# New tokens' scores of a hybrid decoder step, taken out of sixteen decode turns into two blocks of eight heads; value products and the last gate blocks rearranged

## The chip, the cores and the metric

The kernel runs on one core of a Trainium2 chip, in one launch. The metric is device time in microseconds of that core. The engines are TensorE (PE, its weight loads PEld), VectorE (DVE), ScalarE (ACT), GpSimd (POOL) and SyncE (SP), which issues nearly all transfers; instructions on one engine's queue run in their order.

## The reference, cut to what matters

The program is one inference step: a recurrent layer, then a forgetting-attention layer, for a prompt of 2048 tokens and for 8 samples with 8 new tokens each. A sample has 4096 past tokens in 32 cache pages and 16 heads of 64. Its attention is over past and new tokens together:

```
k_all = concat([past_k, k_new]); v_all = concat([past_v, v_new]); c_all = cumsum(logf_all)
s = einsum('bqhd,bkhd->bhqk', q, k) * HEAD_DIM ** -0.5
s = s + cq - ck                       # sums of the log forget gates
s = where(k_pos <= q_pos, s, -inf)
p = softmax(s);  o = einsum('bhqk,bkhd->bqhd', p, v)
y = (o * silu(g)) @ w_out             # q and g come from x @ w_in
```

So each sample has, besides its scores against the cache, an 8x8 block of scores of its new tokens against each other, for each head, with a causal mask.

## The kernel before, in words

The prompt goes through the recurrent layer in two chunks (phase_a1, phase_a2) and through the projections to k, v, q and gate in three (phase_b: 1024, 512 and 512 tokens). Projections of 256 columns are the kv matmuls (token_major) and the qg matmuls (feature_major); every product is three float32r matmuls. The 64 new tokens ride in the first chunk. Their keys and values are stored to DRAM (ks_d, vs_d), their queries too (qs_d), and sample_c stores their forget sums (cn_d).

Decode against the cache is cut into 16 turns, one for a sample and eight heads (DB = 8 samples, 2 groups). The first two turns run beside the projections of the first chunk, the other fourteen beside the projections of the last two chunks and then beside the prompt's attention. Generators yield estimated costs, and Side.along draws decode forward by the cost of the work that it runs beside; a scheduler with a simulated time line then orders each engine's instructions, so the place in the source does not alone decide the place on a queue. The pages come by SyncE (pages, four pages of 256 KB to one raw buffer, four such buffers in the second decode), are transposed on VectorE into ktr (L1193), and meet the queries on TensorE (scores, L1161); the score bank dS is one PSUM bank, tag d. Their sums are subtracted (sc) and the maximum taken.

In the middle of a turn, new_scores (L1169) does the same for the new tokens: the eight key rows lie in rawn (L1116), are transposed into a tile kx that in the second decode is borrowed from the raw ring (spare, shown as sy), 16 matmuls of 8 columns go to a dS bank (L1176), and two VectorE operations take the sums (cn, L1153) off and add the mask maskN; a third takes the maximum (L1182).

Later in the turn the values follow: products (L1275) multiplies four value pages, together keeping the eight matmuls of a buffer in one run, and new_products (L1283) adds the new tokens' rows one tick later, into the same PSUM tile dO. A copy ob is then gathered by four matmuls with the selector sel (L1303, dres).

The gate blocks come last in the last chunk: tanh on ACT (L975) and a product on DVE (L976) into one of two tiles tgb, then a store to sg_d (L977); the last two blocks' stores (cc == 3, that is rows r = 6 and 7) are issued on ACT's queue, all others on SyncE's. Behind them attention opens its PSUM banks (sx, st, ops) over those of the projections, and takes the weight slots (wkept, tags wh0 to wl2) for its accumulators and exponentials.

Of the kernel before, what the change touches and what calls it, by code (L numbers as in the profile page):

```python
# [11 lines left out]
F32 = mybir.dt.float32  # L12
# [3 lines left out]
ALU = mybir.AluOpType  # L16
# [72 lines left out]
def tile_hawk_fox(  # L89
# [102 lines left out]
    c_d = dt_("cd", [2, 4, 4, DB, NPG // 4, 256])  # L192
    cn_d = dt_("cnd", [H, NSAMP])


# [680 lines left out]
    def phase_b(s, x, feed, nk, early, order, opening=None):  # L876
# [7 lines left out]
        with ExitStack() as es:  # L884
# [62 lines left out]
            def feature_major(kind, cc):  # L947

                W = feed.take()
                for fb in range(2):  # L950
                    r = cc * 2 + fb
                    for c0, nn in s.groups:
# [6 lines left out]
                        if kind == "q":  # L959
                            th = pool.tile([P, 512], F32R, name="qth", tag="fth", bufs=2)  # L960
                            tl = pool.tile([P, 512], F32R, name="qtl", tag="ftl", bufs=2)
                            A.mul(th[:, :nn], ps[:, :nn], 0.125)
                            V.scalar_tensor_tensor(tl[:, :nn], ps[:, :nn], 0.125, f(th[:, :nn]),
                                                   op0=ALU.mult, op1=ALU.subtract)
                            S.dma_start(qd_d[r * P:(r + 1) * P, 0, pt:pt + w], f(th[:, so:nn]))
                            S.dma_start(qd_d[r * P:(r + 1) * P, 1, pt:pt + w], f(tl[:, so:nn]))
                            if so:
                                qf = pool.tile([P, NSAMP], F32, name="qf", tag="qf")
                                A.mul(qf[:, :], ps[:, :so], 0.125)
                                for qd in range(4):  # L970
                                    S.dma_start(qs_d[:, :, qd, r, :].rearrange("b j q -> j b q"),
                                                qf[qd * 32:(qd + 1) * 32, :].rearrange("j (b q) -> j b q", b=DB))
                        else:
                            tg = pool.tile([P, 512], F32, name="tgb", tag="tgb", bufs=2)
                            A.activation(tg[:, :nn], ps[:, :nn], AF.Tanh, scale=0.5)  # L975
                            V.scalar_tensor_tensor(tg[:, :nn], tg[:, :nn], 1.0, ps[:, :nn], op0=ALU.add, op1=ALU.mult)  # L976
                            (A if s is scb[-1] and cc == 3 else S).dma_start(sg_d[r * P:(r + 1) * P, pt:pt + w], tg[:, so:nn])  # L977
                            if so:
                                cp(G, sgs[:, r, :], tg[:, :so])
# [24 lines left out]
    def sample_c(pool, lf):  # L1004
# [14 lines left out]
        S.dma_start(cn_d[:, :], cn[:, :])  # L1019

    def drain(gen):
        for _ in gen:
            pass
# [32 lines left out]
    def decode(es, turns, nraw, nktr, ahead):  # L1056
        pool = sbuf(es, "dec", "right")
        maskN = pool.tile([DS, DS], F32, name="maskN")
        G.memset(maskN[:, :], 0.0)
        G.affine_select(maskN[:, :], maskN[:, :], pattern=[[-1, DS]], compare_op=ALU.is_ge, fill=NEG, base=0,  # L1060
                        channel_multiplier=1)
        qmask = pool.tile([P, DS], F32, name="qmask")
# [49 lines left out]

        def new_rows(rows, b, hg):

            assert known >= {("k" if rows is ks_d else "v", hg * 2 + c) for c in range(2)}
            S.dma_start(rawn[:DS, :], rows[b * DS:(b + 1) * DS, hg * 512:(hg + 1) * 512])  # L1116
            return rawn
# [25 lines left out]
        def keys(t, xs):  # L1143
# [24 lines left out]

            def new_scores(raw):  # L1169
                kx = (spare() if ahead else pool.tile([P, 512], F32, name="kx", tag="kx"))[:, :512]  # L1170
                V.transpose(kx, raw[:, :])
                sp = bank("dS")

                def score(h, x):
                    blk = (h * 2 + x) * 32
                    return T.matmul(sp[:32, h * DS:(h + 1) * DS], qw[:, h // 2, h % 2 * 2 + x, :], kx[:, blk:blk + DS],  # L1176
                                    start=(x == 0), stop=(x == 1))

                together([partial(score, h, x) for h in range(8) for x in range(2)])
                tt(V, t.cn[:, :, :], sp[:DS, :64].rearrange("p (h j) -> p h j", h=8), t.cn[:, :, :], ALU.subtract)  # L1180
                tt(V, t.cn[:, :, :], t.cn[:, :, :], maskN[:, :].unsqueeze(1).to_broadcast([DS, 8, DS]), ALU.add)
                V.tensor_reduce(gmx[:DS, 2, :], t.cn[:, :, :], axis=AX.X, op=ALU.max)  # L1182

            for x in xs:
# [78 lines left out]
        def values(t, xs):  # L1263
# [6 lines left out]

            def products(i, raw, came):

# [5 lines left out]

                together([partial(mm, d, a) for d in range(4) for a in range(2)], came, True)

            def new_products(raw):
                for a in range(2):
                    T.matmul(op[a * 32:(a + 1) * 32, :256], pc[:, a * 32:(a + 1) * 32], raw[:, a * 256:(a + 1) * 256],  # L1283
                             start=False, stop=True)

            for x in xs:
                raw, came = t.raws.pop(0) if t.raws else pages(cache_v, b, hg, x)
                dl.after(2 if ahead and x == 0 else 1, lambda i=x * 4, raw=raw, came=came: products(i, raw, came))
                if x == 5:
                    t.rown = new_rows(vs_d, b, hg)  # L1290
# [10 lines left out]
            sp = bank("dres")  # L1301
            for pr in range(4):
                T.matmul(sp[:, pr * 16:(pr + 1) * 16], ob[:, pr % 2 * P:(pr % 2 + 1) * P], sel[:, pr * 16:(pr + 1) * 16],  # L1303
                         start=True, stop=True)
            for h2 in range(2):
# [623 lines left out]
    te1.close()  # L1929
    stage.close()  # L1930
    dec, last = ExitStack(), ExitStack()

# [56 lines left out]
```

## Time and profile before

| what | us |
|---|---|
| three runs | 2989.36, 2994.17, 2994.76 |
| median | 2994.17 |
| profiled execution, its own time | 2990.82 |
| its span, first to last instruction | 2989.1 |
| mean granted TensorE clock | 0.975 |

The page says busy time for each engine, then the chain of work that ended last. A row of the timeline has the start, the duration, the engine, the line, the operation with out<-in, the count, and in brackets how long the engine was idle before it and what ended that. Names are those of tiles; attention's accumulators and exponentials read atth and attl.

### The profile page before, as it was taken

The numbers are of one execution on the slowest core, as the hardware profiler recorded it, in microseconds if no ns is written. First come the engines' busy times: TensorE is split into PE (matmuls) and PEld (weight loads), VectorE is DVE, ScalarE is ACT, GpSimd is POOL, SyncE is SP. The second block draws the span as 40 slices with busy tenths as digits, with TensorE's granted clock in tenths as the row PEclk, the third lists the DMA queues.
The fourth block names the chain that finished last, engine by engine and source line by source line (L and its number), as shares of the span: only waits on it lengthen the run. The fifth ranks groups of instructions, "written<-read, shape, count | busy, mean of one in ns | idle before, by whom it ended". The sixth has DMA issues, their size and how long they took to land.

```text
span 2989.1 us, 60353 instructions
## 1 busy us (share of the span) xinstructions
PE 2794.3 (93%) x21614; PEld 2242.9 (75%) x21614; DVE 1800.4 (60%) x4013; ACT 1266.8 (42%) x2874; POOL 1079.5 (36%) x1198
## 2 busy tenths in 40 slices
PE   5998999999999999999899899989999999899998
PEld 5997789989999987888877665556656666555687
DVE  7877456435257774766554676666766666655344
ACT  4666342222236664443233345344544445355321
POOL 1654111000015541100001265646665666558422
PEclk9999999999999999999999899999999999999999
DMA  4224536789832246899999979887888998773343
GB/s 124 80 89 135 172 122 180 240 259 282 256 98 75 80 154 189 270 316 356 332 323 315 315 228 287 281 267 254 278 297 269 296 283 258 264 256 109 97 149 111
DMA packets 472536, 653.65 MB, mean 219 GB/s; under 512 B 91192, under 2 KB 268601, under 8 KB 464764
## 3 DMA queue, kind: packets, MB, share of 16 engines
q1 hardware_dynamic: 471660, 647.17, 68.0%
q8 instruction: 171, 2.80, 0.4%
q0 software_dynamic: 288, 2.10, 0.3%
q14 instruction: 129, 1.06, 0.1%
q10 hardware_dynamic: 288, 0.52, 0.0%
HBM read 514.09 MB, written 135.16 MB: 217 GB/s over the span
## 4 chain that ended last, share of the span: by engine, by line
PE 45%; DMA 21%; DVE 6%; ACT 4%; SPq 4%; issue 3%; POOL 1%; DVEq 0%; ACTq 0%; POOLq 0%
DMA raw<-in_cache_k_dram 6%; PE ops L1678 6%; PE st L1650 3%; PE sx L1420 3%; PE dO L1275 3%; PE y L384 3%; PE y L385 3%; PE y L386 3%; DMA raw<-in_cache_v_dram 3%; PE st L1651 2%; PE dS L1161 2%; SPq L1106 2%; PE qg L384 2%; PE kv L386 2%; PE kv L385 2%
## 5 line engine op out<-in xcount | busy, mean ns | idle before, releaser
L1193 DVE STREAM_TRANSPOSE ktr<-raw 128x1024 f32<-128x1024 f32 x256 | 307.8, 1225 | 91.2 <-DMA raw<-in_cache_k_dram 78.8
L1422 DVE TENSOR_REDUCE mxs<-sx 128x1 f32<-128x512 f32 x384 | 254.1, 681 | 146.6 <-PE sx L1420 145.4
L384 PE MATMUL kv<-wh,xh 128*128 128x256 f32 (+3 forms) x1088 | 309.4, 288 | 7.7 <-ACT wh L429 5.7
L385 PE MATMUL kv<-wl,xh 128*128 128x256 f32 (+3 forms) x1088 | 309.9, 287 | 2.8 <-DVE wl L430 2.5
L386 PE MATMUL kv<-wh,xl 128*128 128x256 f32 (+3 forms) x1088 | 309.2, 286 | 0.4 <-DMA xl<-xld 0.4
L1665 ACT ACTIVATE atth<-st 128x512 f32<-128x512 f32 (+3 forms) x312 | 171.6, 557 | 208.6 <-PE st L1653 97.1
L1665 ACT ACTIVATE attl<-st 128x512 f32<-128x512 f32 (+3 forms) x300 | 149.7, 507 | 225.7 <-PE st L1651 121.6
L429 ACT ACTIVATE wh<-wst,gv 128x256 fp32r<-128x256 f32 (+1 forms) x384 | 164.5, 499 | 184.6 <-DMA wst<-in_b_w_in_dram 72.4
L430 DVE SCALAR_TENSOR_TENSOR wl<-wst,gv,wh 128x256 fp32r<-128x256 f32 (+1 forms) x384 | 170.7, 494 | 108.5 <-ACT wh L429 108.4
L384 PE MATMUL qg<-xh,wh 128*128 128x384 f32 (+2 forms) x640 | 230.0, 360 | 1.9 <-ACT wh L429 1.9
L385 PE MATMUL qg<-xl,wh 128*128 128x512 f32 (+2 forms) x640 | 228.6, 358 | 0.0
L386 PE MATMUL qg<-xh,wl 128*128 128x384 f32 (+2 forms) x640 | 226.6, 356 | 0.0
L109 POOL TENSOR_TENSOR atth<-atth,atth 128x512 f32<-128x512 f32 (+2 forms) x143 | 168.8, 1180 | 148.6 <-PE ops L1678 82.5
L384 PEld LDWEIGHTS kv<-wh,xh 128*128 128x128 f32 (+1 forms) x1088 | 203.1, 188 | 14.0 <-ACT wh L429 6.4
L385 PEld LDWEIGHTS kv<-wl,xh 128*128 128x128 f32 (+1 forms) x1088 | 203.3, 188 | 8.7 <-DVE wl L430 4.5
L386 PEld LDWEIGHTS kv<-wh,xl 128*128 128x128 f32 (+1 forms) x1088 | 204.5, 188 | 3.4 <-issue 2.6
L109 POOL TENSOR_TENSOR atth<-atth,attl 128x512 f32<-128x512 f32 (+3 forms) x162 | 167.3, 1033 | 41.7 <-PE ops L1678 22.6
L1126 POOL TENSOR_TENSOR qw<-qb,amask 128x128 f32<-128x128 f32 x64 | 31.1, 491 | 411.1 <-PE dS L1161 298.2
L109 POOL TENSOR_TENSOR attl<-attl,atth 128x512 f32<-128x512 f32 (+3 forms) x111 | 129.4, 1166 | 101.0 <-PE ops L1678 63.3
L1275 PE MATMUL dO<-raw,sx 128*32 128x256 f32 x2048 | 139.6, 393 | 27.0 <-DMA raw<-in_cache_v_dram 18.4
L1426 DVE CUSTOM_DVE_ANT_0 sx<-sx,maskb 128x128 f32<-128x128 f32 (+3 forms) x256 | 122.8, 488 | 57.9 <-PE sx L1420 57.3
L919 ACT COPY kf<-kv 128x256 f32<-128x256 f32 (+1 forms) x136 | 49.0, 366 | 226.1 <-PE kv L386 183.3
(354 smaller groups left out, 7519.2 us busy)
## 6 DMA issues: line engine op xcount, KB each, us to landing
raw<-in_cache_k_dram SPq DMA_DIRECT2D x512, 256.0 KB
raw<-in_cache_v_dram SPq DMA_DIRECT2D x512, 256.0 KB
wst<-in_w_kv_dram SPq DMA_DIRECT2D x48, 512.0 KB
wst<-in_b_w_in_dram SPq DMA_DIRECT2D x48, 512.0 KB
xt<-in_x_prompt_dram SPq DMA_DIRECT2D x32, 512.0 KB
wst<-in_a_w_in_dram SPq DMA_DIRECT2D x64, 256.0 KB
out_dram<-kf SPq DMA_DIRECT2D x128, 128.0 KB
sc<-cd SPq DMA_DIRECT2D x16, 1024.0 KB
```

The costliest lines, as they stand in the source:

```text
L109: eng.tensor_tensor(out, a, b, op=op)
L384: T.matmul(ps, lh(k), rh(k), start=(k == 0), stop=False)
L385: T.matmul(ps, lh(k), rl(k), start=False, stop=False)
L386: end = T.matmul(ps, ll(k), rh(k), start=False, stop=(k == nk - 1))
L429: A.activation(wh[:, k, :], st[:, k, :], AF.Copy, scale=gk)
L430: V.scalar_tensor_tensor(wl[:, k, :], st[:, k, :], gk, f(wh[:, k, :]), op0=ALU.mult, op1=ALU.subtract)
L1193: behind("V", V.transpose(t.kts[pp][:, n], raw[:, :, pp * 256:(pp + 1) * 256]).ins)
L1275: return T.matmul(op[c:c + 32, :256], sx[:, d, i // 4, a * 4:(a + 1) * 4, :].rearrange("p h q -> p (h q)"), raw[:, d, a * 256:(a + 1) * 25 ...
L1422: r = V.reduce_max(mx[:, j, ck:ck + 1], ps[:, :w], axis=AX.X)
L1426: V.tensor_tensor_reduce(ps[:, :w], ps[:, :w], maskb[:, 512 - w:], scale=1.0, scalar=NEG, op0=ALU.add, op1=ALU.max, accum_out=mx[:, j, ck: ...
L1665: pair.append((k, lo, p, A.activation(p[:, lo:], ps[:, lo:], AF.Exp)))
L1678: return T.matmul(ops[r * HD:(r + 1) * HD, a0 * P:], vvs[h % 2][:, k, :], p[:, :].rearrange("p (a r c) -> p a r c", a=2, r=2)[:, a0:, r, : ...
```

## The change

It does four things.

1. among_new(pool, hg), new, makes the scores of all 64 new tokens among each other for eight heads: eight transposes of the key rows, eight 64x64 matmuls with the queries (which are now stored once more, as qn_d), the sums off, the mask on, and the result to DRAM (sn_d). It runs once ahead of the first decode (hg 0, three steps of the projections beside it) and once ahead of the second (hg 1, three further steps). Of the 64x64 block only the samples' 8x8 diagonals are read. In a turn, fetch_c loads its 8x8 blocks from sn_d where it loaded the sums, and only the maximum stays; new_scores, kx, maskN and the load of key rows go.
2. The new tokens' value products are the last two matmuls of the run of the last page buffer.
3. The gather takes two matmuls of 32 columns in place of four of 16.
4. The gate blocks with cc == 3 of the last chunk write a tile tgl each, in the weight slot that has been free longest, and their stores go to SyncE.

```diff
+    qn_d, sn_d = dt_("qnd", [D, NSAMP]), dt_("snd", [2, NSAMP, H // 2, NSAMP])
...
+                                S.dma_start(qn_d[r * P:(r + 1) * P, :], qf[:, :])
...
-                            tg = pool.tile([P, 512], F32, name="tgb", tag="tgb", bufs=2)
+                            if opening and cc == 3:
+                                free, i = wslots[0]
+                                tg = free.tile([P, 4 * WC], F32, name="tgl", tag=f"w{'hl'[fb]}{i}")[:, :512]
+                            else:
+                                tg = pool.tile([P, 512], F32, name="tgb", tag="tgb", bufs=2)
...
-                            (A if s is scb[-1] and cc == 3 else S).dma_start(sg_d[r * P:(r + 1) * P, pt:pt + w], tg[:, so:nn])
+                            S.dma_start(sg_d[r * P:(r + 1) * P, pt:pt + w], tg[:, so:nn])
...
+    def among_new(pool, hg):
+
+        h0 = hg * 8
+        kn = pool.tile([NSAMP, 512], F32, name="kn")
+        S.dma_start(kn[:, :], ks_d[:, hg * 512:(hg + 1) * 512])
+        qt = pool.tile([HD, 8, NSAMP], F32, name="qnt")
+        S.dma_start(qt[:, :, :], qn_d[hg * 512:(hg + 1) * 512, :].rearrange("(h d) t -> d h t", d=HD))
+        sn = pool.tile([NSAMP, 8, NSAMP], F32, name="sn")
+        S.dma_start(sn[:, :, :], cn_d[h0:h0 + 8, :].unsqueeze(0).to_broadcast([NSAMP, 8, NSAMP]))
...
+        yield
+        ps = tpp("knt")
+        for h in range(8):
+            T.transpose(ps[:HD, h * NSAMP:(h + 1) * NSAMP], kn[:, h * HD:(h + 1) * HD], ident[:NSAMP, :NSAMP])
+        kt = pool.tile([HD, 8, NSAMP], F32, name="knt")
+        V.tensor_copy(kt[:, :, :].rearrange("d h t -> d (h t)"), ps[:HD, :])
+        yield
+        ps = tpp("snp")
+        for h in range(8):
+            T.matmul(ps[:NSAMP, h * NSAMP:(h + 1) * NSAMP], qt[:, h, :], kt[:, h, :], start=True, stop=True)
+        tt(V, sn[:, :, :], ps[:NSAMP, :].rearrange("q (h t) -> q h t", h=8), sn[:, :, :], ALU.subtract)
+        tt(V, sn[:, :, :], sn[:, :, :], causal[:, :].unsqueeze(1).to_broadcast([NSAMP, 8, NSAMP]), ALU.add)
+        S.dma_start(sn_d[hg], sn[:, :, :])
+        yield
...
-                S.dma_start(t.cn[:, :, :], cn_d[hg * 8:(hg + 1) * 8, b * DS:(b + 1) * DS].unsqueeze(0).to_broadcast([DS, 8, DS]))
+                sl = slice(b * DS, (b + 1) * DS)
+                S.dma_start(t.cn[:, :, :], sn_d[hg, sl, :, sl])
...
-                    t.rown = new_rows(ks_d, b, hg)
...
-                        new_scores(t.rown)
+                        V.tensor_reduce(gmx[:DS, 2, :], t.cn[:, :, :], axis=AX.X, op=ALU.max)
...
+                mms = [partial(mm, d, a) for d in range(4) for a in range(2)]
+                if rown is not None:
+                    mms += [partial(new, a) for a in range(2)]
+                together(mms, came, True)
...
-            dl.after(1, lambda: new_products(t.rown))
...
-            for pr in range(4):
-                T.matmul(sp[:, pr * 16:(pr + 1) * 16], ob[:, pr % 2 * P:(pr % 2 + 1) * P], sel[:, pr * 16:(pr + 1) * 16],
-                         start=True, stop=True)
+            for e in range(2):
+                to, of = (x[:, :64].rearrange("p (a e c) -> p e a c", a=2, e=2)[:, e] for x in (sp, sel))
+                T.matmul(to, ob[:, e * P:(e + 1) * P], of, start=True, stop=True)
...
+    steps(gen, max(0, 36 - done))
+    done = max(done, 36)
+    with ExitStack() as es:
+        for _ in among_new(sbuf(es, "new_0", "right"), 0):
+            steps(gen, 1)
+            done += 1
...
+    with ExitStack() as es:
+        for _ in among_new(sbuf(es, "new_1", "right"), 1):
+            steps(gen, 1)
```

The orders below name a line, an operation, out<-in and its shape; x16 is a run of so many equal rows.

TensorE in a turn beside attention, before: the new tokens' scores (L1176) between the scores st and the maxima sx of attention.

```order
8973 L1650 MATMUL st<-qa_18035,atth 128x512
8974 L1651 MATMUL st<-attl,atth 128x512
8975 L1176 MATMUL dS<-sy,qw 32x8 x16
8976 L1420 MATMUL sx<-atth,qbt_18033 128x512
8977 L1420 MATMUL sx<-atth,qbt_18033 128x384
```

In the changed kernel the new block stands among the projections ahead of the first decode; here its transposes (knt), with the 72 kv matmuls of 128 tokens that end in these rows ahead of them:

```order
2624 L385 MATMUL kv<-wh,xh 128x256
2625 L386 MATMUL kv<-wl,xh 128x256
2626 L387 MATMUL kv<-wh,xl 128x256
2627 L1044 MATMUL knt<-ident,kn 64x64 x8
2628 L385 MATMUL kv<-wh,xh 128x256
```

The runs on dS of 8 columns are in no turn any more, and knt and snp each stand twice in the program.

ScalarE at the joint of projections and attention, before:

```order
927 L975 ACTIVATE tgb<-qg 128x512 x3
928 L1441 ACTIVATE qbt_18034<-mps,st_p 4x128 x4
929 L977 DMA sgd<-tgb 128x512
930 L975 ACTIVATE tgb<-qg 128x512
931 L977 DMA sgd<-tgb 128x512
932 L1665 ACTIVATE atth_19624<-st 128x512
```

And the same place in the changed kernel:

```order
915 L981 ACTIVATE tgl<-qg 128x512
916 L1459 ACTIVATE qbt_17878<-mps,st_p 4x128 x4
917 L981 ACTIVATE tgl<-qg 128x512
918 L981 ACTIVATE tgb<-qg 128x512 x2
919 L1459 ACTIVATE qbt_17879<-mps,st_p 4x128 x4
920 L1683 ACTIVATE atth_19404<-st 128x384
```

The two stores have left ScalarE's queue, and the blocks with tiles of their own stand ahead of the two blocks that came before them.

More of the change, by code (lines that the diff above doesn't have):

```diff
@@ L1167, in scores @@
                 V.tensor_reduce(gmx[:, g, pp * 4:(pp + 1) * 4], sv, axis=AX.XY, op=ALU.max)
[L1169 to L1182, printed above, removed]
             for x in xs:
@@ L1269, in values, with products @@
             op = t.op
-            def products(i, raw, came):
+            def products(i, raw, came, rown=None):
                 def mm(d, a):
@@ L1277, in mm, with new @@
                                     start=(i + d < 2), stop=(i + d == NPG - 1))
[L1279 to L1284, printed above, removed]
+                def new(a):
+                    return T.matmul(op[a * 32:(a + 1) * 32, :256], pc[:, a * 32:(a + 1) * 32],
+                                    rown[:, a * 256:(a + 1) * 256], start=False, stop=True)
+                mms = [partial(mm, d, a) for d in range(4) for a in range(2)]
+                if rown is not None:
+                    mms += [partial(new, a) for a in range(2)]
+                together(mms, came, True)
             for x in xs:
                 raw, came = t.raws.pop(0) if t.raws else pages(cache_v, b, hg, x)
[L1288 removed]
                 if x == 5:
[L1290 removed]
+                    t.rown = new_rows(b, hg)
+                dl.after(2 if ahead and x == 0 else 1,
+                         lambda i=x * 4, raw=raw, came=came, rown=t.rown if x == 7 else None: products(i, raw, came, rown))
                 yield 2 * PV
```

15 lines of the change are left out of this document (8 added, 7 removed).

## The prediction

> **What bounds the kernel now.** I read the page first, then the busy times by stretch, then TensorE's own waits. The page gives the engines and the chain that ended last:
>
> ```profile
> PE 2794.3 (93%) x21614; PEld 2242.9 (75%) x21614; DVE 1800.4 (60%) x4013; ACT 1266.8 (42%) x2874; POOL 1079.5 (36%) x1198
> ...
> PE 45%; DMA 21%; DVE 6%; ACT 4%; SPq 4%; issue 3%; POOL 1%; DVEq 0%; ACTq 0%; POOLq 0%
> ```
>
> TensorE (PE) is busy 93% of the span, and the chain stays on it longest. The 21% on DMA asks for a look by stage. The stretches below are the first two decode turns (500 to 800 us), the rest of the projections with decode beside them (1240 to 1700), and attention with decode beside it (1700 to 2680). Columns: length, busy us of PE, weight loads, DVE, ACT and POOL, then granted clock, DMA share, GB/s.
>
> ```profile
> 500.00:800.00 300.00, 290.24 (x2807) 275.62 (x2806) 119.25 (x223) 79.31 (x212) 7.89 (x28) 0.99 0.83 254
> 1240.00:1700.00 460.00, 429.08 (x3956) 365.98 (x3958) 278.09 (x550) 157.88 (x412) 29.84 (x46) 0.96 1.00 327
> 1700.00:2680.00 980.00, 920.21 (x8506) 586.32 (x8498) 642.07 (x1369) 440.56 (x1097) 588.21 (x565) 0.97 0.85 272
> ```
>
> PE works 93 to 97% of all three. DMA is full only from 1240 to 1700; in attention it has 15% of 980 us, 147 us, to spare. So I take PE as the bound, with DMA close behind in the middle stage. PE's waits that the change touches (total us, times, longest):
>
> ```profile
> PE dO L1275 <- DMA raw<-in_cache_v_dram: 18.4, 14, 3.8
> ...
> PE sx L1420 <- DVE tgb L976: 6.1, 1, 6.1
> ...
> PE dS L1176 <- DVE sc L109: 4.7, 3, 2.5
> ...
> PE st L1650 <- DVE tgb L976: 1.6, 1, 1.6
> ...
> PE dS L1161 <- DVE cn L109: 0.8, 1, 0.8
> ```
>
> **New tokens' scores, removed from the turns.** Each of 16 turns runs 16 small matmuls on L1176, which the trace counts as 32 passes, 512 in all. One turn's, in attention:
>
> ```profile
> 1783.88 0.39 PE L1650 MATMUL st<-qa,atth 128*128 128x512 f32 x1
> 1784.10 0.39 PE L1651 MATMUL st<-attl,atth 128*128 128x512 f32 x1
> 1784.47 1.18 PE L1176 MATMUL dS<-sy,qw 128*32 128x8 f32 x32
> 1785.58 0.68 PE L1420 MATMUL sx<-atth,qbt 96*128 96x512 f32 x2
> ```
>
> A matmul of 512 columns normally takes 0.22 us from start to start (1783.88 to 1784.10). Here the next one comes 1.48 us after 1784.10, so the group costs 1.25 us. Sixteen of them give -20 us; by the bare 1.11 us (1784.47 to 1785.58) it is -18. Both ends are on PE's own time. The waits of L1176 and of L1161 on cn (4.7 + 0.8 us) arise because these scores share the one PSUM bank of the ordinary scores. They can go wholly or be met by the next user of that bank: 0 to -5.5, and I take -3. VectorE loses a transpose of 0.71 us and two small operations per turn, and SyncE a row load. I cost that at nothing: DVE is busy 642 of 980 us in attention. Each turn also stops borrowing one of the four page buffers for the transposed row (the kx tile, in the trace sy). That lets one page load start earlier, and PE's 18.4 us of waits on value pages are what it can shorten: 0 to -5, I take -2.
>
> **Scores of all samples at once, added.** Twice there are 8 transposes (one pass each) and 8 matmuls (two passes), 48 passes. No row has their shape. The nearest are L1176, 1.11/32 = 0.035 us a pass with 32 loaded columns, and L1303 with 128:
>
> ```profile
> 1418.26 0.28 PE L384 MATMUL kv<-wh,xh 128*128 128x256 f32 x1
> 1418.38 0.28 PE L385 MATMUL kv<-wl,xh 128*128 128x256 f32 x1
> 1418.50 0.96 PE L1303 MATMUL dres<-sel,ob 128*128 128x16 f32 x8
> 1419.31 0.36 PE L386 MATMUL kv<-wh,xl 128*128 128x256 f32 x1
> ```
>
> That is 0.81/8 = 0.10 us a pass. With 64 loaded columns I take 0.073, between the two: +3.5 (1.7 to 4.8). Their inputs can add a wait. For the first eight heads the key rows go to DRAM and come back, and PE is queued right behind: in the order, 72 kv matmuls stand between the sample rows' last product and the transposes, 72 x 0.12 = 8.6 us by the rows above. The same trip before took:
>
> ```profile
> 549.57 0.59 SPq L928 DMA_DIRECT2D ksd<-kf  x1
> ...
> 554.95 0.33 SPq L1116 DMA_DIRECT2D rawn<-ksd  x1
> ...
> 559.97 0.71 DVE L1171 STREAM_TRANSPOSE kx<-rawn 128x512 f32<-128x512 f32 x1 [4.45 <-DMA rawn<-ksd]
> ```
>
> From 549.57 to 559.97 are 10.4 us, 2 us more than the cover, and all of PE's projections stand behind that wait: +2.5 (0 to 9; the upper end is 6 us idle and 3 at a lowered clock, as at the joint below). For the second eight the rows have long been stored, and 26 qg matmuls stand between transposes and scores: nothing.
>
> **Value products and the result's gather.** The new tokens' value products keep their passes and only move into the last page's run. Where they stood alone they cost:
>
> ```profile
> 1864.35 0.40 PE L1651 MATMUL st<-attl,kbt 128*128 128x512 f32 x1
> 1864.68 0.63 PE L1283 MATMUL dO<-rawn,dpc 128*32 128x256 f32 x4
> 1865.23 0.50 PE L1650 MATMUL st<-attl,ka 128*128 128x512 f32 x1
> ```
>
> 0.88 less 0.22 is 0.66 us, against 4 x 0.13 when they follow the page products. Four or five of the 16 stood alone, so -0.5. The wait moves too: the last run now needs the new value row, whose load is issued two page groups earlier and covered by them, so I cost it at nothing; uncovered it would add the 18.4/14 = 1.3 us of a page wait to a turn.
>
> On L1303 four matmuls (8 passes, 0.81 us) become two of 32 columns (4 passes). The row's 0.10 us a pass for 16 columns against 0.12 for 256 columns (1418.26 to 1418.38) says that the column count hardly matters, so half goes: 0.40 x 16 = -6.5; if a pass of 32 columns cost 0.12, it would be -5. The Trainium skill, in "TensorE: Matmul & The Clock Gate", section "Back-to-back issue gap", gives small matmuls a floor of about 25 ns each, by which an estimate for the 64 passes that go would be only -1.6 us. Its section "LDWEIGHTS (loading the stationary operand)" makes the time follow the loaded columns, 128 of them here, about 107 ns, and with that the row agrees. I keep -6.5.
>
> **The last two gate blocks.** At the joint to attention, ACT in order of time, then PE, then the joint as one stretch:
>
> ```profile
> 1689.26 0.60 ACT L975 ACTIVATE tgb<-qg 128x512 f32<-128x512 f32 x1 [8.34 <-DMA sgd<-tgb]
> ...
> 1696.32 0.34 ACTq L977 DMA_DIRECT2D sgd<-tgb  x1
> 1696.71 0.60 ACT L975 ACTIVATE tgb<-qg 128x512 f32<-128x512 f32 x1 [5.71 <-DMA atth<-kd]
> ```
>
> ```profile
> 1691.66 0.33 PE L1653 MATMUL st<-attw 128*128 128x128 bf16 x1
> 1698.08 1.22 PE L1420 MATMUL sx<-kbt,qbt 96*128 96x512 f32 x2 [6.09 <-DVE tgb L976]
> ```
>
> ```profile
> 1676.00:1710.00 34.00, 24.02 (x264) 15.90 (x263) 18.32 (x37) 8.29 (x20) 9.76 (x13) 0.70 0.99 315
> ```
>
> Both gate tiles were still being stored, so ACT waited 8.3 us; then the store on ACT's own queue held it 5.7 us. The products sat in PSUM banks that attention needs, and PE stood 10 us in these 34, at a mean clock of 0.70: 24 us of work at 0.70 rather than 1.00 is some 7 us more. With own tiles, and the stores on SyncE, ACT has neither wait; in the new order tgl comes before the two older blocks. The most is -16 or so, the least 0. What is late next: the first sum tile of attention is the same memory as tgl, so its exponential waits for tgl's store, which stands on SyncE's queue behind page loads. In the nearest case that wait was the 8.3 us above, now partly beside scores. I take -9.
>
> **Given back.** In 1240 to 1700 DMA is full, and five turns lie there. Their 5 x 1.65 = 8 us of PE time may only become waits for pages; I take half, +4 (0 to 8).
>
> **Sum:** -20 - 3 - 2 + 3.5 + 2.5 - 0.5 - 6.5 - 9 + 4 = -31 us. The profiled execution took 2990.82 us (span 2989.1 and 1.7 around it), which gives 2960; the median of the three runs, 2994.17, lies 3.4 above it, which gives 2963. I say 2962. The dearest corner of the bounds (-20, -5.5, -5, +1.7, 0, -0.5, -6.5, -16, 0) is -52, which from the median is 2942.
>
> **Rivals.** (1) *PE is not the bound after 1240.* The 14 turns' 14 x 1.65 = 23 us and the 5 us of waits then turn into waits for pages, and there remain the joint (-9), the first two turns (-3) and what is added (+6): -6, which from the profiled execution and the median is 2985 and 2988, say 2986. For it: DMA at 1.00 and pages on the chain; against it: 147 us of free DMA in attention. A rule of the Trainium skill ("Trainium Kernel Development and Optimization", section "Performance Expectations") supports this rival: it calls matmul busy time a poor metric and weight-load busy time a good one. By it PE is at 60% in attention (586 of 980), not 94%. PE's few listed waits speak against it. Chance 0.17. (2) *The joint only changes its wait.* tgl's store sits behind blocked page loads, and the exponential waits as long as ACT did: the -9 is gone, 2971. Chance 0.09. (3) *Slower: the pages start later and DMA sets the pace to 2680.* The second decode now opens after the new block; in the order its first scores come after 104 kv matmuls and not 4, 100 x 0.12 = 12 us later. If DMA were the bound all the way, these 12 us would come one for one, the gain at the joint would be hidden too, and with +2.5 of the first wait and -4 in the first turns the result is +10, 3004. It decides only if DMA cannot catch up 12 us within its 147 spare ones, which speaks against it. Chance 0.05.
>
> **How the numbers follow.** My forecast has 0.69. A measurement of this kernel can tell about 0.2%, 6 us, from no change. The forecast is faster nearly throughout (0.67), rival 1 about six times in ten (0.10), rival 2 nearly always (0.08): faster 0.85; 0.09 falls within 0.2%, mostly rival 1, and 0.06 is slower, mostly rival 3. The range is 2942 to 2986: the dearest corner below, rival 1 above; what it leaves out is rival 3 and the tails of the order that the scheduler drew anew.
>
> **What would show it.** Right: no 32-column passes of 8 columns on PE, L1322 with 64 passes of 0.10 us, PE's busy time down by some 20 us or more, no gap of 6 us at the joint and a clock near 1.00 there. Wrong: PE's busy time falls by 20 us and the span does not (rival 1, with more PE waits on raw); a long wait of the first exponential on the store of tgl (rival 2); the decode's end later against attention than before (rival 3); a wait of the first transposes far above 2 us.

## The result and the profile after

The changed kernel took 2962.66 us in the median of four runs, the kernel before 2994.47 us beside it: a ratio of 0.9893, interval 0.9873 to 0.9914. Measured once more (the run after_again below) it was 0.9921, 0.9899 to 0.9943, that is a gain of 24 us, 17 to 30, where the first measure has 32, 26 to 38. The profiled execution took 2963.43 us with a span of 2961.7. The forecast was 2962, so sign and size came out; not all terms of its sum did, and most of what follows is about that.

The page of the changed kernel, busy times:

```profile
PE 2764.1 (93%) x21086; PEld 2225.5 (75%) x21086; DVE 1785.7 (60%) x3971; ACT 1267.2 (43%) x2874; POOL 1076.4 (36%) x1198
```

The chain of work that ended last is no use here: on the changed kernel's page it reaches back only to 2101 us, so its shares can't be set beside those of before.

TensorE lost 528 passes and 30.2 us of work (2794.3 before), the span 27.4. That looks like one for one, but the stretches say otherwise. The same three as before, in the changed kernel:

```profile
500.00:800.00 300.00, 286.73 (x2733) 273.61 (x2732) 117.85 (x215) 78.02 (x210) 8.07 (x28) 0.99 0.83 254
1240.00:1700.00 460.00, 432.07 (x3830) 369.23 (x3830) 274.20 (x546) 161.49 (x420) 26.93 (x49) 0.96 0.98 324
1700.00:2680.00 980.00, 911.43 (x8268) 577.99 (x8269) 646.46 (x1353) 452.88 (x1123) 606.88 (x581) 0.98 0.86 279
```

In attention TensorE is busy 911 of 980 us where it was 920: some of the freed time became waiting there. Its idle time in all, from 1720 to 2680, is 66.2 us where it was 57.6. TensorE's waits from 1720 to 2680, of the changed kernel, on ACT's exponentials (atth and attl, L1683):

```profile
PE st L1668 <- ACT atth L1683: 10.5, 17, 2.5
...
PE st L1668 <- ACT attl L1683: 5.4, 11, 1.8
...
PE ops L1696 <- ACT atth L1683: 3.8, 7, 2.0
...
PE ops L1696 <- ACT attl L1683: 1.8, 4, 1.1
```

and the same of the kernel before:

```profile
PE st L1650 <- ACT atth L1665: 4.1, 11, 0.8
...
PE ops L1678 <- ACT atth L1665: 3.7, 7, 1.8
PE st L1650 <- ACT attl L1665: 3.2, 6, 1.8
...
PE ops L1678 <- ACT attl L1665: 0.2, 1, 0.2
```

They sum to 21.5 us against 11.2: 10.3 more, where the idle time grew by 8.6 in all. Before 1700 the last matmul of the last projection is where one can compare; first the changed kernel, then the kernel before:

```profile
1679.50 0.40 PE L387 MATMUL qg<-xh,wl 128*128 128x512 f32 x1
```

```profile
1678.32 0.40 PE L386 MATMUL qg<-xh,wl 128*128 128x512 f32 x1
```

Up to here nothing was gained: it ends 1.2 us later, although six turns' scores had been taken out and four gathers halved on the way (the seventh turn's scores of the kernel before and the fifth gather of the changed one stand behind this point). At the joint the 6-us gap is gone, and what is left is one gap on another releaser. The changed kernel's joint:

```profile
1680.10 0.70 PE L1438 MATMUL sx<-kbt,qbt 96*128 96x512 f32 x2
1684.72 0.48 PE L1457 MATMUL mps<-ident,st_s 128*128 128x128 f32 x1 [3.92 <-DVE st_s L1453]
```

```profile
1676.00:1710.00 34.00, 29.97 (x283) 21.37 (x281) 20.85 (x44) 12.00 (x30) 15.48 (x18) 0.85 0.89 282
```

TensorE works 30.0 of these 34 us at a mean clock of 0.85, where it was 24.0 at 0.70. ACT no longer waits there for a gate tile, and the first exponential (L1683) does not wait for the store of tgl: it waits for TensorE's scores. ACT's rows:

```profile
1679.94 0.60 ACT L981 ACTIVATE tgl<-qg 128x512 f32<-128x512 f32 x1 [0.42 <-PE qg L387]
1680.43 1.08 ACT L981 ACTIVATE tgb<-qg 128x512 f32<-128x512 f32 x2
...
1688.33 0.49 ACT L1683 ACTIVATE atth<-st 128x384 f32<-128x384 f32 x1 [1.93 <-PE st L1671]
```

The new block among the projections, and the gather:

```profile
544.10 0.64 PE L1044 MATMUL knt<-ident,kn 64*64 64x64 f32 x8
544.67 0.38 PE L385 MATMUL kv<-wh,xh 128*128 128x256 f32 x1
...
547.94 1.14 PE L1050 MATMUL snp<-knt,qnt 64*64 64x64 f32 x16
549.01 0.39 PE L387 MATMUL kv<-wh,xl 128*128 128x256 f32 x1
```

```profile
690.44 0.53 PE L1322 MATMUL dres<-sel,ob 128*128 128x32 f32 x4
690.80 0.36 PE L387 MATMUL kv<-wh,xl 128*128 128x256 f32 x1
```

The block costs 0.57 and 1.07 us from start to start and nothing waits ahead of it; the gather has 4 passes in 0.36 us.

### The profile page after: what moved, and what is told of

Its sections match the earlier page's. It is cut to its first block, busy times and chain, and to the rows that moved or that the text cites. A ratio compares the mean times of both kernels' runs of the same rounds, so it can differ in the third digit from the quotient of the medians.

```text
span 2961.7 us, 59243 instructions
## 1 busy us (share of the span) xinstructions
PE 2764.1 (93%) x21086; PEld 2225.5 (75%) x21086; DVE 1785.7 (60%) x3971; ACT 1267.2 (43%) x2874; POOL 1076.4 (36%) x1198
## 5 line engine op out<-in xcount | busy, mean ns | idle before, releaser
L1683 ACT ACTIVATE atth<-st 128x512 f32<-128x512 f32 (+3 forms) x312 | 171.4, 557 | 206.0 <-PE st L1671 89.0
L1683 ACT ACTIVATE attl<-st 128x512 f32<-128x512 f32 (+2 forms) x300 | 149.8, 507 | 217.2 <-PE st L1669 122.9
L109 POOL TENSOR_TENSOR atth<-atth,atth 128x512 f32<-128x512 f32 (+3 forms) x143 | 166.9, 1167 | 107.2 <-PE ops L1696 57.9
L1291 PE MATMUL dO<-raw,sx 128*32 128x256 f32 x2048 | 138.2, 391 | 22.1 <-DMA raw<-in_cache_v_dram 16.7
```

Of the source, the lines that this page charges most:

```text
L109: eng.tensor_tensor(out, a, b, op=op)
L1291: return T.matmul(op[c:c + 32, :256], sx[:, d, i // 4, a * 4:(a + 1) * 4, :].rearrange("p h q -> p (h q)"), raw[:, d, a * 256:(a + 1) * 25 ...
L1683: pair.append((k, lo, p, A.activation(p[:, lo:], ps[:, lo:], AF.Exp)))
```

## The experiments

Single executions of the kernel before lay between 2972.9 and 2994.3 us on one chip, so a part's time is read from the ratio with its interval, and a profile, which is one execution, only by what recurs over several kernels. For that I cut each trace at two marks on TensorE: the end of the last projection (qg), and the point at which 2% of attention's 1536 score passes (st) are done. Between them lies the joint; behind it, attention and the output up to TensorE's last matmul (the span goes on for 8.5 to 8.9 us more).

| kernel | ratio to before, interval | last projection ends | joint | rest |
|---|---|---|---|---|
| before | 1 | 1678.7 | 38.6 | 1263.3 |
| order_only | 1.0006, 0.9987 to 1.0024 | 1675.3 | 31.5 | 1261.7 |
| gate_only | 0.9969, 0.9954 to 0.9984 | 1680.1 | 31.6 | 1254.9 |
| gather_only | 0.9940, 0.9918 to 0.9962 | 1673.1 | 38.7 | 1251.5 |
| scores_only | 0.9987, 0.9972 to 1.0001 | 1677.5 | 34.7 | 1255.5 |
| all_but_gate | 0.9975, 0.9954 to 0.9997 | 1677.6 | 41.7 | 1243.1 |
| shared_tile_sync | 0.9952, 0.9933 to 0.9971 | 1684.0 | 37.3 | 1249.5 |
| all_but_scores | 0.9939, 0.9920 to 0.9958 | 1677.6 | 26.8 | 1247.5 |
| after, first profile | 0.9893, 0.9873 to 0.9914 | 1679.9 | 27.6 | 1245.7 |
| after_again | 0.9921, 0.9899 to 0.9943 | 1678.7 | 27.5 | 1250.9 |
| more_mid | 0.9944, 0.9924 to 0.9965 | 1676.0 | 29.8 | 1250.2 |
| more_att | 0.9989, 0.9974 to 1.0003 | 1686.1 | 26.2 | 1256.8 |
| less_decode | 0.9952, 0.9933 to 0.9972 | 1675.4 | 19.6 | 1268.6 |
| least_decode | 0.9909, 0.9885 to 0.9933 | 1641.4 | 20.4 | 1281.0 |

Theory A, formed from the two traces: until the joint DMA sets the time and freed PE work is lost, the joint gives about 11 us by the gate tiles, and attention gives PE time one for one. Theory C is the prediction's sum, in which PE sets the time nearly everywhere. Rival 1 is the prediction's: PE sets nothing after 1240.

**One part alone.** gate_only is the kernel before with this and no more:

```diff
+                            if opening and cc == 3:
+                                free, i = wslots[0]
+                                tg = free.tile([P, 4 * WC], F32, name="tgl", tag=f"w{'hl'[fb]}{i}")[:, :512]
+                            else:
+                                tg = pool.tile([P, 512], F32, name="tgb", tag="tgb", bufs=2)
...
-                            (A if s is scb[-1] and cc == 3 else S).dma_start(sg_d[r * P:(r + 1) * P, pt:pt + w], tg[:, so:nn])
+                            S.dma_start(sg_d[r * P:(r + 1) * P, pt:pt + w], tg[:, so:nn])
```

> The kernel before with the last two gate blocks' own tiles and their stores on SyncE, nothing else. Theory A (the two traces, milestone by milestone: about 11 us were gained at the joint to attention and the rest in attention's turns): -11 us, 2983 (2979 to 2988), ACT's two waits of 8.34 and 5.71 us gone and PE's gap of about 6 us at the first exponentials' scores as well. Theory B (the joint became short only because the turns around it lost work): within 3 us of before, and the first exponential waits for the store of tgl instead.

Measured 2977.02 against 2984.35; by the ratio -9 us (-14 to -5). Theory A's term stands and B falls: the joint gains without the rest of the change.

gather_only is the kernel before with the two-matmul gather:

```diff
-            for pr in range(4):
-                T.matmul(sp[:, pr * 16:(pr + 1) * 16], ob[:, pr % 2 * P:(pr % 2 + 1) * P], sel[:, pr * 16:(pr + 1) * 16],
-                         start=True, stop=True)
+            for e in range(2):
+                to, of = (x[:, :64].rearrange("p (a e c) -> p e a c", a=2, e=2)[:, e] for x in (sp, sel))
+                T.matmul(to, ob[:, e * P:(e + 1) * P], of, start=True, stop=True)
```

> The kernel before with the gather in two matmuls instead of four. Theory A (only the nine turns beside attention pay, 0.41 us each): -3.7 us. Theory C (all sixteen): -6.5 us. The estimate by an issue floor of 25 ns a pass: -1 to -1.6 us. If DMA set the pace: 0. PE's busy time falls by 64 passes in every case.

Measured 2969.47, by the ratio -18 us (-25 to -11): more than any theory allowed.

scores_only is the kernel before with the first of the change's four points alone:

```diff
-                        new_scores(t.rown)
+                        V.tensor_reduce(gmx[:DS, 2, :], t.cn[:, :, :], axis=AX.X, op=ALU.max)
...
+        for _ in among_new(sbuf(es, "new_0", "right"), 0):
...
+        for _ in among_new(sbuf(es, "new_1", "right"), 1):
```

> The kernel before with the new tokens' scores of all samples by eight heads, in place of those in the turns; gather, value products and gate blocks as before. Theory A (nine turns of 1.25 us pay; what is added costs 1.65 us once in the first projections and nothing in the DMA-full stretch): -10 us (-7 to -12). Theory C (sixteen turns of 1.25, 5 us of waits less, 3.3 us added): -20 us (-17 to -22). Rival 1: +2 to 0.

Measured 2980.19, by the ratio -4 us (-8 to 0): far less than C, and between A's -7 to -12 and rival 1's +2 to 0. The place of the loss shows in TensorE's waits from 1720 to 2680 of scores_only:

```profile
PE st L1662 <- ACT atth L1677: 14.0, 19, 3.6
...
PE st L1662 <- ACT attl L1677: 5.5, 11, 1.7
...
PE ops L1690 <- ACT atth L1677: 1.9, 6, 0.6
...
PE ops L1690 <- ACT attl L1677: 0.6, 2, 0.3
```

22.0 us, as in the changed kernel. Over the table's first twelve kernels these waits are 10 to 13 us in the five that keep the turns' scores, 19 to 24 in six of the seven that don't, and 12.2 in the seventh, more_att, which has other work there in their place. Grouped by tile, the dS passes behind the second mark took 85.5 to 87.8 us in the five kernels that keep the turns' scores and 74.1 to 76.3 in the seven others of the table's first twelve, 11 us less, and the waits on exponentials grew by about that much.

**The change without one part.** all_but_gate undoes point 4 and all_but_scores point 1 of the change.

```diff
-                            if opening and cc == 3:
-                                free, i = wslots[0]
-                                tg = free.tile([P, 4 * WC], F32, name="tgl", tag=f"w{'hl'[fb]}{i}")[:, :512]
-                            else:
-                                tg = pool.tile([P, 512], F32, name="tgb", tag="tgb", bufs=2)
+                            tg = pool.tile([P, 512], F32, name="tgb", tag="tgb", bufs=2)
...
-                            S.dma_start(sg_d[r * P:(r + 1) * P, pt:pt + w], tg[:, so:nn])
+                            (A if s is scb[-1] and cc == 3 else S).dma_start(sg_d[r * P:(r + 1) * P, pt:pt + w], tg[:, so:nn])
```

> The changed kernel with the last two gate blocks as before (two shared tiles, the last stores on ACT's queue). Theory A (turns in the DMA-full stretch give nothing, the nine turns beside attention give 1.65 us each): -15 us against before, 2979 (2975 to 2984), with ACT's wait on the gate's stores back. Theory C (all sixteen turns pay one for one, and the waits on the shared bank go too): -20 to -25 us, 2969 to 2974. Rival 1 of the prediction (PE is not the bound after 1240): -3 us or less.

Measured 2974.58, -7 us by the ratio (-14 to -1): a smaller gain than A's -15. Its joint is the worst of all. TensorE, then ACT, in all_but_gate:

```profile
1699.32 0.79 PE L1664 MATMUL st<-qa,ka 128*128 128x512 f32 x1 [17.13 <-DVE tgb L978]
```

```profile
1697.31 1.23 ACT L977 ACTIVATE tgb<-qg 128x512 f32<-128x512 f32 x2 [13.93 <-DMA sgd<-tgb]
```

Against after_again the part that is left out is worth some 16 us here (0.9975 against 0.9921). With the intervals of both that is 7 to 25, so it can't be told from the 9 (5 to 14) that it is worth alone.

```diff
-                        V.tensor_reduce(gmx[:DS, 2, :], t.cn[:, :, :], axis=AX.X, op=ALU.max)
+                        new_scores(t.rown)
...
-        for _ in among_new(sbuf(es, "new_0", "right"), 0):
...
-        for _ in among_new(sbuf(es, "new_1", "right"), 1):
```

> The changed kernel with the new tokens' scores in the turns as before (its gather, value products and gate tiles are the changed ones). Theory A (PE time one for one beside attention, the joint by the own tiles): -8 at the joint and -5 for eleven gathers, -13 us against before, and the scores are then worth the other 10. If the gather is worth the 15 us of its own run: -23 us or more, and the scores nothing.

Measured 2964.54 against 2987.12; by the ratio -18 us (-24 to -13), between A's -13 and the -23 that the gather's own run would give. Gather, value products and gate tiles alone make most of the gain. With 9 us for the gate tiles, some 9 are left for the other two, half of what gather_only had, though the intervals overlap. With the turns' scores still there, its waits on exponentials from 1720 to 2680 are as short as those of the kernel before, 10.3 us:

```profile
PE st L1656 <- ACT atth L1671: 6.5, 12, 2.0
...
PE st L1656 <- ACT attl L1671: 1.8, 7, 0.4
...
PE ops L1684 <- ACT atth L1671: 1.5, 4, 0.8
...
PE ops L1684 <- ACT attl L1671: 0.5, 2, 0.3
```

**Tile or queue.** shared_tile_sync is the changed kernel with the shared tiles back, but the stores left on SyncE.

```diff
-                            if opening and cc == 3:
-                                free, i = wslots[0]
-                                tg = free.tile([P, 4 * WC], F32, name="tgl", tag=f"w{'hl'[fb]}{i}")[:, :512]
-                            else:
-                                tg = pool.tile([P, 512], F32, name="tgb", tag="tgb", bufs=2)
+                            tg = pool.tile([P, 512], F32, name="tgb", tag="tgb", bufs=2)
```

> The changed kernel with the last two gate blocks in the two shared tiles, but all stores on SyncE: the queue alone. If the shared tiles make the joint's wait: a gap on TensorE at the first scores of attention that ends on a gate tile, 6 to 17 us, and 5 to 15 us more than the changed kernel. If ACT's own stores made it: no such gap, and the time of the changed kernel.

Measured 2972.65, -14 us by the ratio (-20 to -9), with the gap. TensorE, then ACT, in shared_tile_sync:

```profile
1700.66 0.80 PE L1664 MATMUL st<-qa,ka 128*128 128x512 f32 x1 [12.11 <-DVE tgb L978]
```

```profile
1698.66 1.22 ACT L977 ACTIVATE tgb<-qg 128x512 f32<-128x512 f32 x2 [8.90 <-DMA sgd<-tgb]
```

The shared tiles make the wait, whichever queue stores them. Own tiles with the stores on ACT weren't tried.

**The whole once more.** after_again is the changed kernel, without an edit, measured beside the next three.

> The changed kernel once more, on the chip of the other runs of this call and with more repetitions, as the measure for the parts. All theories: -1.07% as in the first comparison, -27 to -38 us; a part's gain can only be set against this number, since the kernel before itself spread from 2972.9 to 2994.3 us in the last comparison.

Measured 2962.06 against 2985.13: a gain of 24 us where the first comparison had 32, somewhat below the 27 to 38 that were expected. The changed kernel took the same time both times, the kernel before 9 us less this time.

**The order by itself.** order_only is the kernel before with another step cost in the planner:

```diff
-    QK, PV, HOP = 700.0, 255.0, 300.0
+    QK, PV, HOP = 705.0, 255.0, 300.0
```

> The kernel before with one number of its planner changed, the cost of a step of two key transposes from 700 to 705, which computes the same with the same instructions in a partly different order (4306 lines of difference on TensorE). Theory L (a new order by itself is worth as much as the small parts: the gather alone gave -15 us where its PE time is 6.5, the scores alone -4 where theirs is 16): 5 to 10 us away from before, either way. Theory P (the parts' times are their own work): within 3 us of before.

Measured 1.0006 (0.9987 to 1.0024): this other order is worth nothing that can be told, within 7 us, and theory L is left only with +5 to +7. It does move the joint, where the gap at a shared tile was 6.1 us before and is

```profile
1685.94 0.50 PE L1650 MATMUL st<-qa,ka 128*128 128x512 f32 x1 [2.52 <-DVE tgb L976]
```

in order_only, against

```profile
1693.97 1.33 PE L1420 MATMUL sx<-kbt,qbt 96*128 96x512 f32 x3 [11.87 <-DVE tgb L976]
```

in gather_only. With shared tiles the gap is 2.5 to 17.1 us as the order falls; with own tiles no pass of attention waits for a gate tile there. Over the table's first twelve kernels the joint takes 31.5 to 41.7 us with shared tiles (mean of six 37.1) and 26.2 to 31.6 with own ones (mean of six 28.2): 9 us. The two ranges touch, order_only's 31.5 with shared tiles and gate_only's 31.6 with own ones.

**PE work added, by stage.** more_mid and more_att are the changed kernel with the gather repeated, with the same result, in some turns of the second decode (t.it is the turn's number in it). more_mid has

```diff
+                self.it = it
...
-            for e in range(2):
+            for e in (0, 1) * (13 if ahead and t.it < 3 else 1):
```

> The changed kernel with the gather of the three turns that end in the DMA-full stretch (1240 to 1700) issued 13 times over instead of once: 24 further matmuls a turn of 0.18 us, by the gather's own row (2 in 0.36 us), 72 in all, 13 us of PE time. Theory A (that stretch is set by DMA): +4 us or less against the changed kernel. Theory C (PE sets it): +13 us (10 to 16).

Measured 2966.27 against 2962.06 for after_again beside it: +4 us by the medians, +7 by the ratios, of the 13 that were meant to be added (in the trace the added passes take 20 us, some of them at a lowered clock). In the trace the last projection ends no later than without (1676.0). The stretch 1200 to 1680, in more_mid and then in the changed kernel:

```profile
1200.00:1680.00 480.00, 465.62 (x4006) 403.97 (x4004) 291.18 (x620) 178.08 (x452) 24.78 (x55) 0.98 0.96 320
```

```profile
1200.00:1680.00 480.00, 455.99 (x3894) 392.44 (x3891) 289.99 (x618) 178.07 (x456) 21.39 (x50) 0.98 0.97 321
```

TensorE took 10 us of work more without ending later (from 1200 to 1676, where it ends, it is 461.6 against 452.0). But this is the work of only two of the three turns. The third turn's passes stand behind the last projection, most of them in one run in the joint, which is 2 us longer than without:

```profile
1678.56 6.01 PE L1323 MATMUL dres<-sel,ob 128*128 128x32 f32 x32
```

So by this trace the 4 to 7 us are not the price of the full stretch. The waits that the two turns filled are those which the change had opened. Those on query tiles in the changed kernel, 8.6 us where the kernel before has 1.2:

```profile
PE kv L385 <- DVE qtl L964: 4.5, 1, 4.5
PE qg L385 <- DVE qtl L964: 4.1, 2, 3.0
```

are 3.2 us in more_mid. Over the table's first twelve kernels, from 1200 to 1680, they are 0 to 2.5 us in the five that keep the turns' scores and 8.1 to 10.3 in the six others besides more_mid. Behind them stands DMA: ACT can't write the next query tile before the store of the last one has landed; VectorE waits for the weights that ACT does next, and then has other work ahead of its part of the query tile; and TensorE meanwhile lacks the PSUM bank. In the changed kernel, ACT, VectorE and then TensorE:

```profile
1558.88 0.60 ACT L963 ACTIVATE qth<-qg 128x512 fp32r<-128x512 f32 x1 [4.57 <-DMA qd<-qth]
...
1559.91 1.28 DVE L431 SCALAR_TENSOR_TENSOR wl<-wst,gv,wh 128x256 fp32r<-128x256 f32 x3 [8.41 <-ACT wh L430]
```

```profile
1564.50 0.58 PE L385 MATMUL kv<-wh,xh 128*128 128x256 f32 x1 [4.47 <-DVE qtl L964]
```

more_att has

```diff
+                self.it = it
...
-            for e in range(2):
+            for e in (0, 1) * (5 if ahead and t.it >= 3 else 1):
```

> The changed kernel with the gather of the eleven turns that end beside attention issued five times over instead of once: 8 further matmuls a turn of 0.18 us, 88 in all, 16 us of PE time. Theories A and C (PE sets attention's time): +16 us (12 to 20) against the changed kernel. Rival 1 of the prediction (DMA sets it): +4 us or less.

Measured 2979.72, +17.7 us against after_again, which speaks against rival 1. It is not clean support for one for one, though. In the trace the gather's passes take 26.9 us behind the second mark instead of 6.0, and only 6 to 11 us of these 21 appear in the rest (1256.8 against 1245.7 and 1250.9); 6 to 7 us stand in the projections, which this order made longer. The waits on exponentials are back at 12.2 us. TensorE's waits from 1720 to 2680 in more_att:

```profile
PE st L1669 <- ACT atth L1684: 6.3, 14, 1.7
...
PE ops L1697 <- ACT atth L1684: 4.1, 9, 1.3
...
PE st L1669 <- ACT attl L1684: 1.3, 5, 0.4
...
PE ops L1697 <- ACT attl L1684: 0.5, 2, 0.3
```

So added work in attention fills these waits, as removed scores open them.

**Decode moved out of the full stretch.** less_decode and least_decode are the changed kernel with

```diff
-SHARE = 1.13
+SHARE = 1.05
```

> The changed kernel with one number of the planner changed, decode's share of the steps beside the projections from 1.13 to 1.05, so that some of decode's work and page traffic moves from the DMA-full stretch (1240 to 1700) into attention, where DMA has 11 to 16% free. Theory A (the stretch is set by DMA and absorbs PE work, attention is set by PE): the last projection ends earlier by 10 to 20 us and attention gets longer by the PE time moved, about 7% of the stretch's decode, 8 to 12 us; in sum 0 to -10 us against the changed kernel. Theory C (PE sets both): 0, the ends shift and the sum stays. A slower one, by 5 us or more, would mean that attention has no DMA to spare.

and with 0.97:

> The same with 0.97: the ends move twice as far. Theory A: -5 to -15 us as long as PE still waits in the stretch, then no more. Theory C: 0. If attention's DMA fills up, slower.

less_decode took 2973.54 us, by the ratios some 9 more than after_again: the projections end only 3 to 5 us earlier, the joint is 8 us shorter, and the rest is 18 to 23 us longer. least_decode took 2955.46; its interval overlaps with that of after_again (0.9885 to 0.9933 against 0.9899 to 0.9943), so it can't be told from it. Its projections end 37 to 39 us earlier and the rest takes 30 to 35 longer. What attention does with more pages, in least_decode from 1720 to 2680:

```profile
PE dO L1291 <- DMA raw<-in_cache_v_dram: 32.2, 19, 5.7
```

That is 32 us of waits on value pages, where the changed kernel has 13.4 in the same window. The 147 us of free DMA are no reserve that TensorE can use without waiting for pages.

## Why the prediction was right, and where its steps were not

The total came out, but there is luck in it. The scores with all that hangs on them (-20, -3, -2, +3.5, +2.5 and +4) stand in the sum with -15 and brought -4 (-8 to 0) alone. The other three parts stand with -16 and brought -18 (-24 to -13) together, in all_but_scores. That makes -22, close to the 24 us of the second measure and short of the first's 32, which met the forecast's 31. Where the rest of those 32 comes from, if it is there, no run shows.

**New scores, -20 and -3 and -2.** This term was mis-sized, and the step that failed is "Both ends are on PE's own time". The passes went as priced (the dS rows lost 11 us in attention, nine turns of 1.25), but their place in attention had covered the wait for ACT's exponentials, which rose from 11.2 to 21.5 us; and in the full stretch the freed time became waits for stores, 8.6 us where there were 1.2. Alone the scores gave -4 us (-8 to 0). Waits on the shared bank went from L1176 to the page scores (L1193 in the changed kernel; on sc 4.7 us became 3.3), and those on value pages stayed (18.4 and 16.7). A busy engine with few long waits still had many short ones ready to grow: the prediction listed only the waits of the lines that it changed.

**Blocks added, +3.5 and +2.5.** 1.64 us a block by the first block's rows, 3.3 for both, as priced; the wait for the round trip didn't come, nothing being idle ahead of the transposes.

**Gather, -6.5.** Its busy time fell from 16.0 to 8.7 us, as worked out from the 0.10 us a pass; a pass of 32 columns took 0.36 / 4 = 0.09 us. The floor of about 25 ns that the Trainium skill gives in "TensorE: Matmul & The Clock Gate", section "Back-to-back issue gap", would by an estimate have made it 1.6; the row decided against it rightly. But alone it brought -18 us (-25 to -11), though all_but_scores, which has it beside the gate tiles, brought no more. In the two kernels with this gather and the turns' scores the rest was 1251.5 and 1247.5 us, against 1254.9 to 1263.3 in the three with neither part: about 10 us, of which 5 are its own passes in attention. Where the others come from is open; order_only shows that a new order can be worth nothing, not that this one is.

**Value products, -0.5.** Not measured by itself; it is below what a comparison tells.

**Gate blocks, -9.** Right in size, and in mechanism for the shared tiles: 9 us over twelve traces, 9 us alone. The second wait, 5.7 us that the prediction laid to the store on ACT's own queue, isn't shown to matter: its row names a DMA of keys (atth<-kd) as what ended it, and shared_tile_sync has the gap with no store on that queue. What rival 2 foresaw, an exponential that waits for the store of tgl, didn't occur in the changed kernel and stayed small in more_mid, where ACT has at the joint

```profile
1687.84 0.98 ACT L1684 ACTIVATE atth<-st 128x512 f32<-128x512 f32 x2 [1.80 <-DMA sgd<-tgl]
```

against the 8.3 us that it was priced at. The clock there was 0.85, not near 1.00.

**Given back, +4.** Undersized. From the first kv matmul of the last chunks (1198 to 1206) to the last projection's end lie 474 to 481 us in ten of the table's first twelve traces (gather_only 472, more_att 485), whatever was taken out. All of the 8 us and the waits were given back, not half, and the first turns' 3 us can't be seen at the last projection either.

**Rivals.** Rival 1 fits the stretch from 1240 to 1700, where 10 us of added work didn't move the last projection's end. Behind that stretch more_att speaks against it: the added work took 17.7 us where its price was 16, though only 6 to 11 of them stand behind the joint. For the scores alone it was not far off (+2 to 0, where -4 came), but by another wait: the time that was freed in attention became waits for exponentials, not for pages. The rule in the Trainium skill, "Trainium Kernel Development and Optimization", section "Performance Expectations", that matmul busy time is a poor metric, agrees with the full stretch, where TensorE was 95% busy (455.99 of 480) and yet took 10 us of work more without ending later; its better metric, weight-load busy, stood at 82% there (392.44 of 480) and at 59% in attention (577.99 of 980), where added work did cost time, so by itself it would have misled here. Rival 3 didn't occur: the second decode's end came 24.5 us earlier, not later (its last result on TensorE ends at 2650.3, before at 2674.8).

**By parts**, the ratios sum to -9 - 18 - 4 = -31 us, against -24 (-30 to -17) and -32 us measured for the whole. Within the intervals the parts add up. The widest difference is that of gather and gate tiles: -27 as a sum of the two alone, -18 together with the value products in all_but_scores. It too is no larger than the noise allows.

## What to carry to other kernels

A small operation between large ones may be paid for by a wait that it covers: before counting its time as gain, look at what the engine would wait for next in its place, and sum the many short waits of the neighbours, not only those of the lines touched. Ask this by stage: the one that is full of transfers gave nothing back here, and a few matmuls put into it for trial told so, once it was looked up where the scheduler had put them. Two buffers at the end of a stage whose stores queue behind other transfers make a wait whose length is a matter of the order (2.5 to 17 us here); in the eight kernels with own buffers no pass of attention waited for one there.

## What the runs showed of the hardware

The granted clock stayed halved for a while after a gap at the changed kernel's joint. In steps of 2 us, with TensorE's busy time first behind the comma and the clock in the third column from the end:

```profile
1682.00:1684.00 2.00, 0.00 (x0) 0.00 (x0) 2.00 (x6) 0.00 (x0) 1.94 (x2) 0.63 0.87 345
1684.00:1686.00 2.00, 1.28 (x5) 0.76 (x5) 0.67 (x3) 0.70 (x3) 1.89 (x5) 0.50 1.05 339
...
1690.00:1692.00 2.00, 2.00 (x20) 1.40 (x23) 2.00 (x5) 1.26 (x3) 0.00 (x0) 0.50 1.06 181
```

TensorE was back at 1684.7 and full again by 1686, but the clock was 0.50 until 1692 (0.81 in the next step): 3.9 us idle went with some 8 us of work at half clock. Behind the gap of 17.1 us in all_but_gate it was shorter: work came back at 1699.3, and the window 1702 to 1704 already had 0.71, the next 1.00.

That the gap is the cause isn't shown. In more_mid the third turn's repeated gather fills the same place, TensorE is busy all through, and the clock is halved for as long:

```profile
1680.00:1682.00 2.00, 2.00 (x11) 2.00 (x11) 0.16 (x1) 0.00 (x0) 1.89 (x5) 0.50 0.96 390
...
1686.00:1688.00 2.00, 2.00 (x7) 1.51 (x7) 1.58 (x4) 0.20 (x2) 0.00 (x0) 0.50 1.05 406
```

The run of 32 gather passes took 5.82 us from start to start there, 0.18 us a pass, where the 20 passes just ahead of it, at a clock of 1.00, took 0.11. So filling the gap with these small passes did not keep the clock up here.
